# Rotary embedding on one core: a first store that begins with 1 KB of each partition

## The chip, the cores and the metric

The kernel runs on one core of one Trainium2 chip. The metric is the device time of one execution in microseconds (us); the median of several runs is compared.

## The reference

A rotary position embedding. `x` has 16 batches of 512 positions of 16 heads of 64 numbers, all float32 (33.5 MB); `cos` and `sin` have 512 x 32 numbers (64 KB each).

```python
x = x.reshape(batch, seq, num_heads, head_dim)
x1, x2 = x[..., :half_dim], x[..., half_dim:]
cos = cos[None, :, None, :]
sin = sin[None, :, None, :]
rotated = np.concatenate([x1 * cos - x2 * sin,
                          x1 * sin + x2 * cos], axis=-1)
```

So 33.5 MB are read, 33.5 MB are written, and each number takes part in two products and one sum.

## The kernel before

The 16 batches are worked on as 8 slabs of two batches' size. A slab is 128 partitions by 8192 float32, 4 MB. Two neighbouring slabs (0-1, 2-3, 4-5, 6-7) make a pair: a partition holds 64 KB of the pair, which lie next to each other in the input and in the output, and partition p's row lies 64 KB behind that of partition p-1. There are three places on the chip for a pair (`places`, the tile named `pair` in the profile), so pair 6-7 goes into the place of pair 0-1 once that is stored.

`load(s, n, parts)` brings n slabs from slab s on into their place, `store` writes them to the output; both are issued by SyncE (line 66 in the profile, where `issue` records every DMA) in the order of the program. That order is: load 0 (4 MB), cos, sin, loads 1, 2 and 3 (4 MB each), load 4-5 (8 MB); then store 0-1 in two halves, the even partitions and the odd ones, and load 6-7 in the same two halves; then stores 2-3, 4-5 and 6-7, 8 MB each. Half of load 6-7 can start when the half of store 0-1 that reads the same partitions has landed. SyncE takes its instructions one after the other: one that waits holds all behind it.

Ahead of all that ScalarE issues two DMAs of 512 bytes (line 85): from the tile `blank`, which holds zeros, to the start of the output, which store 0-1 overwrites later, and from the start of `cos` into another part of `blank`.

The tables for cos and sin are loaded into every fourth partition, spread over all partitions by eight small matmuls and kept in bfloat16 (`tabs`). A slab is then worked on in place: ScalarE casts it to bfloat16 into the lower half of its own bytes (line 154), VectorE multiplies it by the two tables (line 170, two instructions) and adds the products crosswise (line 173), and ScalarE casts the sum back to float32 (line 154). The cast of slab s+1 comes ahead of the products of slab s. Slab 0 is done in two passes and slab 7 in three, so that the first can begin and the last end early; the others are done in one. After the last cast of an odd slab, its pair is stored.

Of the kernel before, what the change touches and what calls it, by code (L numbers as in the profile page):

```python
# [2 lines left out]

# [4 lines left out]


@with_exitstack  # L10
def kernel(
    ctx: ExitStack,
    tc: tile.TileContext,
    x: bass.AP,
    cos: bass.AP,
    sin: bass.AP,
    num_heads: int,
    out: bass.AP,
):
    nc = tc.nc  # L20
    P = nc.NUM_PARTITIONS

    batch, seq, dim = x.shape
    nh = num_heads
    hd = dim // nh
    half = hd // 2
    bf16 = mybir.dt.bfloat16
    f32 = mybir.dt.float32

    nb = 2  # L30
    nslabs = batch // nb
    rpp = nb * seq // P
    W = rpp * dim
    TP = seq // (2 * rpp)
    TS = P // TP
    TW = 2 * rpp * half

    out_flat = out.rearrange("b s h d -> b s (h d)")

    singles = ctx.enter_context(tc.tile_pool(name="singles", bufs=1))  # L40
    pairs = ctx.enter_context(tc.tile_pool(name="pairs", bufs=3))
    psum = ctx.enter_context(tc.tile_pool(
        name="psum", bufs=1, space=bass.MemoryType.PSUM))


    def view(t, offset, *dims):
        return dataclasses.replace(t, offset=t.offset + offset,
                                   ap=[t.ap[0], *[list(d) for d in dims]])

    places = [pairs.tile([P, 2 * W], f32, tag="pair", name="pair") for _ in range(3)]


    def here(s, n=1):
        return view(places[s // 2 % 3], s % 2 * W, (1, n * W))


    def there(t, s, n=1):  # L60
        return bass.AP(tensor=t.tensor, offset=t.offset + s // 2 * 2 * P * W + s % 2 * W,
                       ap=[[2 * W, P], [1, n * W]])


    def issue(out, in_):
        tc.keep_in_program_order(nc.sync.dma_start(out=out, in_=in_))  # L66


    def load(s, n=1, parts=slice(None)):
        issue(here(s, n)[parts], there(x, s, n)[parts])  # L70


    def store(s, n=1, parts=slice(None)):
        issue(there(out_flat, s, n)[parts], here(s, n)[parts])


    EVEN, ODD = slice(0, P, 2), slice(1, P, 2)


    blank = singles.tile([1, 2 * P], f32, tag="blank")  # L80
    nc.vector.memset(view(blank, 0, (1, P)), 0.0)  # L81
    for i, t in enumerate((out_flat, cos)):
        far = bass.AP(tensor=t.tensor, offset=t.offset, ap=[[P, 1], [1, P]])
        near = view(blank, i * P, (1, P))
        tc.keep_in_program_order(nc.scalar.dma_start(
            out=near if i else far, in_=far if i else near))

    load(0)


    cos_sb = singles.tile([P, TW], f32, tag="cos_sb")
    sin_sb = singles.tile([P, TW], f32, tag="sin_sb")
    for t, src in ((cos_sb, cos), (sin_sb, sin)):
        nc.vector.memset(t, 0.0)  # L94
        issue(t[::TS], bass.AP(
            tensor=src.tensor, offset=src.offset, ap=[[TW, TP], [1, TW]]))

    load(1)
    load(2)
    load(3)  # L100
    load(4, 2)


    pick = singles.tile([P, 2 * P], bf16, tag="pick")
    nc.gpsimd.memset(pick, 0.0)  # L105
    for g in range(2):
        part = view(pick, g * P, (TP, P // TP), (1, TP))
        nc.gpsimd.affine_select(  # L108
            out=part, in_=part, compare_op=mybir.AluOpType.not_equal,
            fill=1.0 - 2.0 * g, base=0, pattern=[[0, P // TP], [-TS, TP]],  # L110
            channel_multiplier=1)

    tab1 = singles.tile([P, 2 * TW], bf16, tag="tab1")
    for i, t in enumerate((cos_sb, sin_sb)):
        nc.vector.tensor_copy(out=view(tab1, i * TW, (1, TW)), in_=t)  # L115

    accs, tabs = [], []
    for h in range(2):
        acc = psum.tile([P, 2 * rpp * hd], f32, tag=f"acc{h}", name="acc")
        for i in range(2):  # L120
            for f in range(2):
                nc.tensor.matmul(  # L122
                    view(acc, i * rpp * hd + f * half, (hd, rpp), (1, half)),
                    view(pick, i * f * P, (1, P)),
                    view(tab1, i * TW + h * rpp * half, (half, rpp), (1, half)),
                    start=True, stop=True)
        accs.append(acc)
        tabs.append(singles.tile([P, 2 * rpp * hd], bf16, tag=f"tab{h}", name="tab"))
    nc.vector.tensor_copy(out=tabs[0], in_=accs[0])  # L129

    passes = []
    for s in range(nslabs):
        r = 0
        for n in {0: (4, 4), nslabs - 1: (4, 2, 2)}.get(s, (rpp,)):
            passes.append((s, r, n))
            r += n


    def halves(u):
        s, r, n = u
        t = here(s).bitcast(bf16)
        return [view(t, (2 * r + i * n) * dim, (1, n * dim)) for i in range(2)]


    def cast(u):
        s, r, n = u
        copy(halves(u)[0], view(here(s), r * dim, (1, n * dim)))  # L150


    def copy(out, in_):
        tc.keep_in_program_order(nc.scalar.copy(out=out, in_=in_))  # L154


    for i, u in enumerate(passes):
        s, r, n = u
        if i == 0:
            cast(u)  # L160
            cast(passes[1])
            copy(tabs[1], accs[1])
            cast(passes[2])
        elif s > 0:
            for v in passes:
                if v[0] == s + 1:
                    cast(v)
        lo, up = halves(u)
        for t, a in ((up, 0), (lo, rpp * hd)):
            nc.vector.tensor_mul(  # L170
                out=t, in0=lo,
                in1=view(tabs[s % 2], a + r * hd, (hd, n), (0, nh), (1, hd)))
        nc.vector.tensor_add(  # L173
            out=up, in0=up, in1=view(lo, half, (hd, n * nh), (-half, 2), (1, half)))

        copy(view(here(s), r * dim, (1, n * dim)), up)
        if s == 1:
            for act in (store, load):
                for parts in (EVEN, ODD):
                    act(0 if act is store else 6, 2, parts)  # L180
        elif s % 2 and r + n == rpp:
            store(s - 1, 2)


# [1 line left out]
_INS = ['x', 'cos', 'sin', 'num_heads']  # L186
_OUTS = [((16, 512, 16, 64), 'float32')]

_NUMBERS = {'num_heads': 16}


# [26 lines left out]
```

## Time and profile before

| | |
|---|---|
| median of 3 runs | 162.09 us (161.96 to 162.14) |
| the profiled execution | 162.06 us, its span 160.3 us |
| ScalarE busy | 113.9 us (71%) |
| VectorE busy | 109.8 us (68%) |
| TensorE busy | 1.9 us (1%) |
| moved by DMA | 67.24 MB in 1572 packets, 420 GB/s over the span |

The span runs from the first to the last instruction of the program; the time of the execution also holds what lies around it. The profile calls the queue of SyncE's DMAs q1 and that of ScalarE's q10. SPq, ACTq and PEq are the instruction queues of SyncE, ScalarE and TensorE. A DMA is cut into packets, one for each partition's row here, which the 16 DMA engines move; a window's "DMA share" is the mean busy share of these engines, with each packet put where it begins, so that short windows show some unevenness (shares over 1). A packet of 4 bytes at the end of a DMA on each engine reports its completion. "Landing" is the time when all 16 reports of a DMA are in.

### The profile page before, as it was taken

Reading aid. Unit: us, or ns where it says so; the run is one execution under the profiler, and the core shown is the slowest. Engines: PE = TensorE matmul, PEld = TensorE weight load, DVE = VectorE, ACT = ScalarE, POOL = GpSimd, SP = SyncE. Lnnn points to the kernel's source line nnn. Section 1 sums busy time; section 2 is a strip of 40 time slices with the busy share of each in tenths; the row PEclk is TensorE's granted clock in tenths of the full one; section 3 lists DMA queues with packets and bytes.
Section 4 is the critical chain, followed back from the end, with each engine's and each line's share of the span. In section 5 each row is a group of like instructions: output and inputs, shape, how many; then the busy total and the mean of one; then the engine's idle time right before and its main releaser. Section 6 shows DMA issues by size and latency. Waiting matters only on the chain.

```text
span 160.3 us, 176 instructions
## 1 busy us (share of the span) xinstructions
PE 1.9 (1%) x8; PEld 1.1 (1%) x8; DVE 109.8 (68%) x39; ACT 113.9 (71%) x24; POOL 1.1 (1%) x7
## 2 busy tenths in 40 slices
PE   0004000000000000000000000000000000000000
PEld 0002000000000000000000000000000000000000
DVE  2004899999899989989998996008999998000000
ACT  3008959999999999999999900699999969400000
POOL 2000000000000000000000000000000000000000
DMA  7999999999989996996996997997997998998983
GB/s 262 393 393 450 499 393 393 499 417 393 540 376 523 393 393 262 523 507 278 523 507 278 523 474 311 523 474 311 523 458 327 523 425 360 523 409 376 523 376 147
DMA packets 1572, 67.24 MB, mean 420 GB/s; under 512 B 226, under 2 KB 228, under 8 KB 292
## 3 DMA queue, kind: packets, MB, share of 16 engines
q1 hardware_dynamic: 1568, 67.24, 98.0%
q10 hardware_dynamic: 4, 0.00, 0.0%
HBM read 33.69 MB, written 33.55 MB: 420 GB/s over the span
## 4 chain that ended last, share of the span: by engine, by line
DMA 44%; ACT 18%; DVE 15%; issue 7%; ACTq 2%; SPq 1%
DMA pair<-in_x_dram 24%; DMA out_dram<-pair 19%; ACT pair L154 18%; DVE pair L170 10%; DVE pair L173 4%; ACTq L213 1%; SPq L66 1%; DVE sin_sb L94 0%; DVE cos_sb L94 0%; DVE blank L81 0%; ACTq L154 0%
## 5 line engine op out<-in xcount | busy, mean ns | idle before, releaser
L154 ACT CAST pair<-pair 128x8192 bf16<-128x8192 f32 (+5 forms) x22 | 111.7, 5153 | 22.5 <-DMA pair<-in_x_dram 21.1
L170 DVE TENSOR_TENSOR pair<-pair,tab 128x8192 bf16<-128x8192 bf16 (+2 forms) x22 | 71.4, 3259 | 12.7 <-ACT pair L154 12.4
L173 DVE TENSOR_TENSOR pair<-pair 128x8192 bf16<-128x8192 bf16 (+2 forms) x11 | 35.8, 3259 | 0.3
L115 DVE CAST tab<-cos_sb 128x512 bf16<-128x512 f32 x1 | 0.4, 428 | 11.0 <-DMA cos_sb<-in_cos_dram 11.0
L154 ACT ACT_TABLE_LOAD x1 | 1.3, 1283 | 1.8 <-DVE cos_sb L94 1.8
L122 PE MATMUL acc<-tab,pick 128*128 128x256 bf16 x8 | 1.9, 411 | 13.6 <-DVE tab L115 13.6
L129 DVE CAST tab<-acc 128x1024 bf16<-128x1024 f32 x1 | 1.2, 1225 | 1.0 <-PE acc L122 1.0
L122 PEld LDWEIGHTS <-pick 128*128 128x128 bf16 x8 | 1.1, 136 | 13.9 <-issue 12.0
L154 ACT CAST tab<-acc 128x1024 bf16<-128x1024 f32 x1 | 1.0, 1004 | 0.0
L81 DVE MEMSET blank<- 1x128 f32 x1 | 0.2, 165 | 0.8 <-PEq L199 0.8
L108 POOL TENSOR_SCALAR_AFFINE_SELECT pick<-pick 128x128 bf16<-128x128 bf16 x2 | 0.6, 308 | 0.1
L94 DVE MEMSET sin_sb<- 128x512 f32 x1 | 0.5, 485 | 0.1
L94 DVE MEMSET cos_sb<- 128x512 f32 x1 | 0.5, 485 | 0.1
L115 DVE CAST tab<-sin_sb 128x512 bf16<-128x512 f32 x1 | 0.4, 420 | 0.0
L105 POOL MEMSET pick<- 128x256 bf16 x1 | 0.3, 311 | 0.3 <-POOLq L199 0.3
L199 POOL MEMSET const-bfloat16-1.0<- 128x1 bf16 x1 | 0.1, 101 | 0.0
L199 POOL MEMSET const-uint8-127<- 128x1 uint8 x1 | 0.1, 101 | 0.0
L199 POOL MEMSET const-float32-0.0<- 128x1 f32 x1 | 0.1, 98 | 0.2 <-issue 0.2
L199 POOL MEMSET const-float32-1.0<- 128x1 f32 x1 | 0.1, 98 | 0.0
## 6 DMA issues: line engine op xcount, KB each, us to landing
pair<-in_x_dram SPq DMA_DIRECT2D x4, 4096.0 KB, 24.6
out_dram<-pair SPq DMA_DIRECT2D x5, 24.6
cos_sb<-in_cos_dram SPq DMA_DIRECT2D x1, 64.0 KB, 11.4
sin_sb<-in_sin_dram SPq DMA_DIRECT2D x1, 64.0 KB, 11.0
pair<-in_x_dram SPq DMA_DIRECT2D x3, 19.3
out_dram<-blank ACTq DMA_DIRECT2D x1, 0.5 KB
blank<-in_cos_dram ACTq DMA_DIRECT2D x1, 0.5 KB
```

What stands on the lines that cost most here:

```text
L66: tc.keep_in_program_order(nc.sync.dma_start(out=out, in_=in_))
L94: nc.vector.memset(t, 0.0)
L105: nc.gpsimd.memset(pick, 0.0)
L108: nc.gpsimd.affine_select(out=part, in_=part, compare_op=mybir.AluOpType.not_equal, fill=1.0 - 2.0 * g, base=0, pattern=[[0, P // TP], [-T ...
L115: nc.vector.tensor_copy(out=view(tab1, i * TW, (1, TW)), in_=t)
L122: nc.tensor.matmul(view(acc, i * rpp * hd + f * half, (hd, rpp), (1, half)), view(pick, i * f * P, (1, P)), view(tab1, i * TW + h * rpp * ...
L129: nc.vector.tensor_copy(out=tabs[0], in_=accs[0])
L154: tc.keep_in_program_order(nc.scalar.copy(out=out, in_=in_))
L170: nc.vector.tensor_mul(out=t, in0=lo, in1=view(tabs[s % 2], a + r * hd, (hd, n), (0, nh), (1, hd)))
L173: nc.vector.tensor_add(out=up, in0=up, in1=view(lo, half, (hd, n * nh), (-half, 2), (1, half)))
L199: nc = _bacc.Bacc("TRN2", target_bir_lowering=False, num_devices=1)
L213: with _tile.TileContext(nc) as tc:
```

## The change

Store 0-1 becomes three DMAs in place of two: first the first 256 numbers (1 KB) of the 64 KB of each of the 128 partitions, then the remaining 63 KB of the even partitions, then those of the odd ones. Load 6-7 stays in two halves; each writes whole rows, so the even half now needs the 1 KB store and the even store to have landed, and the odd half the 1 KB store and the odd store. To this end `here`, `there`, `load` and `store` take a range `a` to `b` within the row. The 512 byte read of `cos` on ScalarE's queue is left out; the 512 byte write to the output stays.

```diff
-    def here(s, n=1):
-        return view(places[s // 2 % 3], s % 2 * W, (1, n * W))
+    def here(s, n=1, a=0, b=None):
+        b = n * W if b is None else b
+        return view(places[s // 2 % 3], s % 2 * W + a, (1, b - a))
...
-    def store(s, n=1, parts=slice(None)):
-        issue(there(out_flat, s, n)[parts], here(s, n)[parts])
+    def store(s, n=1, parts=slice(None), a=0, b=None):
+        issue(there(out_flat, s, n, a, b)[parts], here(s, n, a, b)[parts])
...
-    blank = singles.tile([1, 2 * P], f32, tag="blank")
-    nc.vector.memset(view(blank, 0, (1, P)), 0.0)
-    for i, t in enumerate((out_flat, cos)):
-        far = bass.AP(tensor=t.tensor, offset=t.offset, ap=[[P, 1], [1, P]])
-        near = view(blank, i * P, (1, P))
-        tc.keep_in_program_order(nc.scalar.dma_start(
-            out=near if i else far, in_=far if i else near))
+    SHORT = 256
+    blank = singles.tile([1, P], f32, tag="blank")
+    nc.vector.memset(blank, 0.0)
+    tc.keep_in_program_order(nc.scalar.dma_start(out=bass.AP(
+        tensor=out_flat.tensor, offset=out_flat.offset, ap=[[P, 1], [1, P]]), in_=blank))
...
         if s == 1:
-            for act in (store, load):
-                for parts in (EVEN, ODD):
-                    act(0 if act is store else 6, 2, parts)
+            store(0, 2, b=SHORT)
+            for parts in (EVEN, ODD):
+                store(0, 2, parts, a=SHORT)
+            for parts in (EVEN, ODD):
+                load(6, 2, parts)
```

## The prediction

> **What bounds the kernel now.** I read the page first, then SyncE's waits, then the time by windows, then the packet records of the trace.
>
> ```profile
> span 160.3 us, 176 instructions
> ...
> PE 1.9 (1%) x8; PEld 1.1 (1%) x8; DVE 109.8 (68%) x39; ACT 113.9 (71%) x24; POOL 1.1 (1%) x7
> ...
> q1 hardware_dynamic: 1568, 67.24, 98.0%
> q10 hardware_dynamic: 4, 0.00, 0.0%
> HBM read 33.69 MB, written 33.55 MB: 420 GB/s over the span
> ```
>
> No compute engine is above 71%, but queue q1 (all DMAs that SyncE issues) keeps the 16 DMA engines busy for 98.0% of the span. The packet records say the same from inside. Each engine starts at 1.8 to 2.4 us, then runs packet after packet with no gap until 158.4 to 159.1 us; a 64 KB packet takes 2.418 us, a 32 KB packet 1.213 us. The sum for one engine: 32 x 1.213 + 48 x 2.418 = 154.9, cos and sin with the completion packets 0.5, and 1.7 of excess that I come to, together 157.1 us, which is 98.0% of 160.3. So this is one stream of transfers, and the time changes only by what lengthens, shortens or starves that stream. 1.8 us lie around the span (162.06 for the profiled execution; the median of the three runs is 162.09, so the two agree).
>
> Does anything starve it? SyncE's waits:
>
> ```profile
> SPq L66 <- ACT pair L154: 91.4, 3, 37.5
> SPq L66 <- DMA out_dram<-pair: 29.9, 2, 20.6
> ...
> SPq L66 <- DMA pair<-in_x_dram: 8.5, 1, 8.5
> ```
>
> and its issues in the timeline:
>
> ```profile
> 50.71 1.16 SPq L66 DMA_DIRECT2D out_dram<-pair  x2
> ...
> 72.53 10.48 SPq L66 DMA_DIRECT2D pair<-in_x_dram  x2
> ...
> 83.11 55.39 SPq L66 DMA_DIRECT2D out_dram<-pair  x3
> ```
>
> The two halves of store 0-1 are issued at 50.71 and 51.3, but the stream is busy with load 4-5 and begins them at 62. The even half has landed at 72.5; load 6-7 even is issued then, 9 us before the stream has finished the odd half. Load 6-7 odd follows at 82.50, 9 us ahead as well, then store 2-3 at 83.11, 18 us ahead. These waits are long but covered.
>
> What is left to win is the excess. The windows (length, busy times, clock, DMA share, GB/s):
>
> ```profile
> 41.60:51.30 9.70, 0.00 (x0) 0.00 (x0) 9.10 (x3) 9.70 (x3) 0.00 (x0) 1.00 1.01 439
> ...
> 58.50:62.10 3.60, 0.00 (x0) 0.00 (x0) 3.57 (x2) 3.60 (x1) 0.00 (x0) 1.00 0.82 291
> 62.10:64.50 2.40, 0.00 (x0) 0.00 (x0) 2.40 (x1) 2.40 (x2) 0.00 (x0) 1.00 1.01 437
> ...
> 100.80:103.20 2.40, 0.00 (x0) 0.00 (x0) 0.00 (x0) 1.62 (x1) 0.00 (x0) 1.00 1.01 437
> ```
>
> From 58.5 to 62.1 the stream carries 291 GB/s where its neighbours carry 437. In the packet records these are the last packets of load 4-5, one on each of the 16 engines: 3.16 to 4.03 us, mean 3.59, in place of 2.42. All engines lose about 1.17 us, right ahead of the first packet of the first large store. The next turn from load to store, at 101, shows nothing (437). The other excess is at the start: the first 32 KB packet of each engine takes 1.72 in place of 1.21.
>
> **The change, part by part.**
>
> *Short store, as bytes.* Store 0-1 moves the same 8 MB. What is new is 128 packets of 1 KB, 8 for each engine. From the records, a 512 B packet took 27 ns and a 2 KB packet 84, so 0.0371 ns a byte and 8 ns fixed; 1 KB makes 46 ns. Eight are 0.37 us, plus a completion packet of 9 ns; the 8 KB that they take out of the large packets save 8 x 2.418/64 = 0.30. Net +0.08 us. A second row supports it: the loads of cos and sin, 128 KB in 2 KB packets, took 4 x 84 + 2 x 9 = 0.35 us on an engine against 0.30 at full rate. The same bytes in more packets cannot take less, so the low end is the 0.05 of the row above (a gain by the slow packet is counted below); the high end is that pieces of 1 KB written to rows 64 KB apart go badly, for which the nearest row is the slow packet, +1.2. I take 0.08, since the 512 B packet that fits the line was itself a write to the output.
>
> [...]
>
> *Short store, as an issue.* One more DMA on SyncE, some 0.5 us (two took 1.16 us), at 50.7. The even and odd halves go out at 51.2 and 51.8; the stream reaches them at 62, so 10 us hide it. Without that cover it costs 0.5.
>
> *Short store, as a wait.* Load 6-7 even must now wait for the short store and for the even half. The short one ends first, and the even half some 0.23 us later than now (0.38 of short packets less 0.15 by its four shorter rows). Behind the waiting instruction stand load 6-7 odd and store 2-3, both with 9 us or more. Cost 0.
>
> *The slow packet.* This is the part that can move the time. If the 1.17 us come from the size of the first store packet that the engines take up while the last load packet still runs, a 1 KB packet cuts them: down to -1.2. If they are a fixed cost of the first large write, they stay, and a second small-to-large step could bring a second one: +1.2. For a fixed cost: all 16 engines end the slow packet within 0.7 us (61.8 to 62.5) whenever they began it, and the turn at 101 with the same packet sizes shows nothing, so it is not size alone. I take 0.
>
> *No short read of cos.* Two packets of 27 and 9 ns on one engine, 0.04 us, and one issue of 0.23 us on ScalarE's queue at 1.54, ahead of an activation table load that ends 9.7 us before ScalarE's first data. Gain 0 to 0.04. The unknown is whether the small read at 6 us makes the real cos load at 12.0 us go smoothly: its packets show no excess. Bounds for a cold first read: nothing, up to 0.5 (start of x) or 1.2 (first store). The read went through one engine only, and sin, which nobody reads ahead, shows no excess either. I take 0.
>
> *A side effect.* Load 4-5 is the ninth DMA issued now, and SyncE waits 8.5 us for load 0 before it, although its place is empty: the DMAs seem to share eight completion semaphores in turn. With the read gone it is the eighth, and goes out near 4.7 us rather than 12.8. The stream has loads until 42 us; cost 0.
>
> *The end.* Store 6-7 is issued at 138.17 and the stream finishes store 4-5 at 139.8. The chain of waits behind that issue begins with the landing of load 6-7 odd at 101.5, which is in the same stream just ahead of stores 2-3 and 4-5, so both shift together and the 1.6 us stay.
>
> Sum: 162.06 + 0.08 - 0.00 = 162.14, call it 162.2. That is within 0.2% (0.3 us), about what a measurement of this kernel can tell from no change.
>
> **The rivals.**
>
> B, faster: the slow packet shrinks. For: it stands exactly ahead of the first large store, where the change puts small packets, and the first packets of 32 KB lost 0.5 us where the 64 KB ones lost 1.2. Against: the clustered ends and the clean turn at 101. Time 162.06 + 0.08 - 0.4 to 1.2 = 160.9 to 161.7.
>
> C, slower: the first read of cos becomes cold. The place is 12 us, between load 0 and load 1; the price 0.5 to 1.2 us on every engine, as at the start of x and of the first store; it decides as soon as load 0's last packet takes over 1.5 us. For: the clean 2 KB packets now follow a small read of the same tensor by 6 us. Against: the small write to the output at 3.6 us did not keep the first store clean, and sin is clean without help. Time 162.6 to 163.3.
>
> D, slower: the stall stays and the 1 KB writes, or the step from them to 63 KB packets, cost up to as much again: 162.5 to 163.3. Against: the 27 ns write.
>
> E, slower: load 6-7 even is held until the odd half has landed too, because the short store touches all partitions. Then the stream runs dry: 0.36 from last packet to landing, 1.02 from issue to first packet (0.73 to 1.75 at the start), 0.5 for the slow first packet, 1.9 together: 164.0. Against: the even half does not wait for the odd one today.
>
> F, slower: the short store pays its own start and landing in the stream, 1.02 + 0.36 = 1.4: 163.5. Against: cos and sin follow each other with no gap.
>
> **How the numbers follow.** A (nothing moves, 162.0 to 162.4) 0.32; B 0.30; C 0.20; D 0.10; E 0.05; F 0.03. Faster is B, 0.30; same is A, 0.32; slower is C to F, 0.38. The time is A's. The range of 8 in 10 takes in B, A, C and D, 160.9 to 163.4, and leaves out E, F and the ends of the others; A's own range is 162.0 to 162.4.
>
> **What would show it.** Right: the window ahead of the first store still near 291 GB/s; queue q1 with 1712 packets (1568 + 128 + 16), q10 with 2; load 4-5 issued near 4.7 us; load 6-7 even near 72.7; every window after 62 at 437; span near 160.4. B shows as that window at 400 or more and all later issues of SyncE about 1 us earlier. C shows as a dip at 11 to 13 us with load 0 landing late; D as a dip after 62; E as load 6-7 even issued near 82.6. Far outside would be 63 KB rows cut into many pieces: q1 with thousands of packets.

## The result and the profile after

The changed kernel takes 162.44 us (median of 9 runs, 162.32 to 162.62), the kernel before 162.03 (161.90 to 162.33) beside it: a ratio of 1.0025, 95% interval 1.0016 to 1.0033. It is slower by 0.4 us. The profiled execution took 162.39 us with a span of 160.2.

The page of the changed kernel:

```profile
span 160.2 us, 178 instructions
...
PE 1.9 (1%) x8; PEld 1.1 (1%) x8; DVE 109.7 (69%) x39; ACT 113.9 (71%) x24; POOL 1.1 (1%) x7
...
q1 hardware_dynamic: 1712, 67.24, 98.0%
q10 hardware_dynamic: 2, 0.00, 0.0%
```

The span is no longer than before: 160.2 against 160.3. The counts of packets are the forecast ones. What is longer is the time outside the span: 162.39 - 160.21 = 2.18 us here, 162.06 - 160.27 = 1.79 before.

SyncE's waits and its issues in the timeline:

```profile
SPq L68 <- DMA out_dram<-pair: 29.6, 2, 20.5
...
SPq L68 <- DMA pair<-in_x_dram: 8.1, 1, 8.1
```

```profile
2.75 2.09 SPq L68 DMA_DIRECT2D pair<-in_x_dram  x4
...
33.49 18.50 SPq L68 DMA_DIRECT2D out_dram<-pair  x3
...
72.55 10.20 SPq L68 DMA_DIRECT2D pair<-in_x_dram  x2
...
82.83 55.62 SPq L68 DMA_DIRECT2D out_dram<-pair  x3
```

Load 4-5 now goes out with loads 1 to 3 (four issues from 2.75 on, the last at 4.4). The short store goes out at 33.49, which I had put at 50.7: its 256 numbers lie in the first pass of slab 0, whose cast back ends then. The wait of 8.1 us for load 0 is now ahead of it. The early issue gains nothing, since the stream reaches the store at 62 either way. The two halves follow at 50.84 and 51.4; load 6-7 even is issued at 72.55, as before at 72.53.

The windows (length, busy times, clock, DMA share, GB/s), with the first one over the last packets of load 4-5:

```profile
58.30:61.75 3.45, 0.00 (x0) 0.00 (x0) 3.45 (x1) 3.45 (x1) 0.00 (x0) 1.00 0.98 304
62.05:64.45 2.40, 0.00 (x0) 0.00 (x0) 2.37 (x2) 2.40 (x1) 0.00 (x0) 1.00 1.08 459
...
100.80:103.20 2.40, 0.00 (x0) 0.00 (x0) 0.00 (x0) 1.67 (x1) 0.00 (x0) 1.00 1.01 437
```

The first window in the trace of before:

```profile
58.30:61.75 3.45, 0.00 (x0) 0.00 (x0) 3.45 (x1) 3.45 (x1) 0.00 (x0) 1.00 1.04 304
```

The slow packet is still there, but windows this short don't show it safely: a packet counts where it begins, and the prediction's own window, 58.5 to 62.1, gives 185 GB/s here. So the reading rests on the packet records. In them it takes 3.38 us on the mean of the 16 engines (3.60 before). The 1 KB packets take 46 ns each and the 63 KB ones 2.380 us, with no gap between them. So the stream is what the sum made of it, and the 0.4 us are not in it.

### The profile page after: what moved, and what is told of

It is laid out like the page before. It is cut to its first block, busy times and chain, and to the rows that moved or that the text cites. A ratio compares the mean times of both kernels' runs of the same rounds, so it can differ in the third digit from the quotient of the medians.

```text
span 160.2 us, 178 instructions
## 1 busy us (share of the span) xinstructions
PE 1.9 (1%) x8; PEld 1.1 (1%) x8; DVE 109.7 (69%) x39; ACT 113.9 (71%) x24; POOL 1.1 (1%) x7
## 4 chain that ended last, share of the span: by engine, by line
DMA 44%; ACT 18%; DVE 15%; issue 7%; ACTq 2%; SPq 1%
DMA pair<-in_x_dram 25%; DMA out_dram<-pair 19%; ACT pair L154 18%; DVE pair L170 10%; DVE pair L173 4%; ACTq L215 1%; SPq L68 1%; DVE sin_sb L94 0%; DVE cos_sb L94 0%; DVE blank L84 0%; ACTq L154 0%
```

## The experiments

In what follows "outside" is the time of a run less its span, as a mean over the 11 or 12 runs of each kernel; the kernel before has 1.79 in each of the four comparisons (15 to 35 runs each, single runs 1.74 to 1.84; the spans of single runs are on record to 0.1 us, which alone makes such a spread). A trace also holds instructions that only wait for semaphores (EVENT_SEMAPHORE), which the page does not count, and on VectorE three named DRAIN; with them VectorE has 53 in the kernel before and 55 in the changed one, and no other engine has a different number (SyncE 33, ScalarE 45, GpSimd 23).

**The two parts of the change, one by one.** *e1_no_read* is the kernel before without the read of cos:

```diff
-    for i, t in enumerate((out_flat, cos)):
...
-        tc.keep_in_program_order(nc.scalar.dma_start(
-            out=near if i else far, in_=far if i else near))
+    tc.keep_in_program_order(nc.scalar.dma_start(out=bass.AP(
+        tensor=out_flat.tensor, offset=out_flat.offset, ap=[[P, 1], [1, P]]), in_=blank))
```

> The kernel before without the short read of cos; store 0-1 stays in two halves of 64 KB rows. If the change's 0.4 us come with the dropped read (theory R), this run is near 162.4 with a span near 160.2, the difference lying outside the span. If they come with the short store (theory S), it is at 162.0 with 160.3. If only the number of instructions or DMAs matters (theory N), it is at or under 162.0.

Measured: ratio 1.0007 (0.9997 to 1.0016), outside 1.78, span 160.49 where before had 160.44.

*e2_short_and_read* is the changed kernel with that read kept:

```diff
-    tc.keep_in_program_order(nc.scalar.dma_start(out=bass.AP(
-        tensor=out_flat.tensor, offset=out_flat.offset, ap=[[P, 1], [1, P]]), in_=blank))
+    for i, t in enumerate((out_flat, cos)):
...
+        tc.keep_in_program_order(nc.scalar.dma_start(
+            out=near if i else far, in_=far if i else near))
```

> The kernel before with the short store of 1 KB of each partition and its two 63 KB halves, the short read of cos kept. Theory R: 162.0 to 162.1 (span 160.2 to 160.4, about 1.8 outside). Theory S: near 162.4. Theory N: at or over 162.4, with one DMA more than either kernel.

Measured: ratio 1.0025 (1.0015 to 1.0034), outside 2.19, span 160.45 where before had 160.44.

*e3_change_again* is the changed kernel, unedited.

> The changed kernel itself, unedited, beside the others on the same chip: 162.4 by every theory, span 160.2 to 160.3, about 2.15 outside the span. If it is at 162.0 here, the difference belongs to the chip and not to the program.

Measured: ratio 1.0023 (1.0014 to 1.0031), outside 2.20, span 160.38.

So the difference comes with the short store and lies outside the span; the dropped read costs nothing that these runs can tell. Theory R (the dropped read) falls. Against the kernel before, e2_short_and_read has one more instruction on SyncE (the DMA), one on ScalarE (a wait) and two on VectorE; in the changed kernel, which lacks the read, SyncE and ScalarE stand at the numbers of before. So what both slower kernels have more is one DMA with its packets, and two VectorE instructions.

**Which of these it is.** VectorE's line 170, before and after:

```profile
L170 DVEq EVENT_SEMAPHORE  x6: 21/21/1256, 14.8 to 101.5; - x6
```

```profile
L170 DVEq EVENT_SEMAPHORE  x8: 21/21/1256, 14.9 to 108.6; - x8
```

The products on slab 6 wait for DMAs that used its place. By the semaphores that the trace records there, these are the two halves of load 6-7 in the kernel before, in one waiting instruction; with the short store they are these two and all three DMAs of store 0-1, in three instructions. The two more take 21 and 50 ns, inside the span, and are hidden: VectorE waits there for ScalarE's cast in either kernel. Three kernels change the number of instructions without the short store, or the other way about.

*e4_two_on_vector*:

```diff
     nc.vector.tensor_copy(out=tabs[0], in_=accs[0])
+    spare = singles.tile([1, P], f32, tag="spare")
+    for _ in range(2):
+        nc.vector.memset(spare, 0.0)
```

> The kernel before with two more tiny VectorE instructions (writes of zeros to an unused tile, 0.17 us each, behind the tables), no short store. In the first runs the time outside the span was 1.79 us in the kernel before and without the read (53 VectorE instructions in the trace) and 2.19 with the short store (55), the spans alike. Theory V (VectorE's number of instructions adds the 0.4): 2.19 outside, 162.5 to 162.6 on this chip, ratio 1.0025. Theory D (the short DMA itself adds it): 1.79 outside, 162.2. Theory T (the number of all instructions, 178 here): 2.19.

Measured: ratio 1.0001 (0.9992 to 1.0010), outside 1.79. It decides nothing: the two instructions ran from 2.0 us on, ahead of the casts of cos and sin, the two waiting instructions in front of these casts fell away, and the trace has 53 on VectorE again.

*e5_two_on_gpsimd* is the same edit with `nc.gpsimd.memset`.

> The kernel before with the same two tiny instructions on GpSimd instead, 178 instructions in all and 53 on VectorE. Theory V: 1.79 outside the span, 162.2. Theory D: 1.79, 162.2. Theory T: 2.19, 162.6.

Measured: ratio 0.9998 (0.9989 to 1.0007), outside 1.79, 178 instructions in all. The number of all instructions (theory T) is not it.

*e6_change_two_fewer* is the changed kernel with

```diff
-    nc.vector.memset(blank, 0.0)
+    nc.gpsimd.memset(blank, 0.0)
...
-        nc.vector.memset(t, 0.0)
+        (nc.vector if t is cos_sb else nc.gpsimd).memset(t, 0.0)
```

> The changed kernel with two fewer VectorE instructions: the zeroing of blank and of sin_sb is done by GpSimd. Theory V: 1.79 outside the span, and as the span is that of the changed kernel (160.2 to 160.4), 162.1 to 162.2, level with the kernel before or 0.05 us under it. Theory D and theory T: 2.19 outside, 162.6, ratio 1.0025.

Measured: ratio 0.9997 (0.9988 to 1.0007), outside 1.79, span 160.48 where before had 160.44. Its line 170 still has the eight waits:

```profile
L170 DVEq EVENT_SEMAPHORE  x8: 21/21/1256, 14.9 to 108.9; - x8
```

The short store and its waits are all there, VectorE has 53 instructions, and the 0.4 us are gone. That takes out the DMA itself (theory D) and leaves VectorE's number of instructions.

**The number alone.** Copies of one number per partition, placed behind the tables in a fixed order so that they take over no wait (n = 2, 1 and 8):

```diff
+    spare = singles.tile([P, n], f32, tag="spare")
+    for k in range(n):
+        tc.keep_in_program_order(nc.vector.tensor_copy(
+            out=view(spare, k, (1, 1)), in_=view(tabs[0], k, (1, 1))))
```

> The kernel before with two more VectorE instructions (copies of one number per partition to an unused tile) placed so that they take over no wait: 55 in the trace, as in the changed kernel; two halves of store 0-1, no short store. Theory V (the number of VectorE instructions): 2.19 us outside the span, 162.6 on a chip where before is 162.2, ratio 1.0025. Theory W (it is not the number, but the waits on the short store's completion): 1.79 outside, 162.2.

Measured (*e8_vector_55*): ratio 1.0022 (1.0014 to 1.0030), outside 2.21, span 160.28 where before had 160.34. Its line for the products, which is line 174 there:

```profile
L174 DVEq EVENT_SEMAPHORE  x6: 21/21/50, 16.2 to 101.7; - x6
```

Theory V is shown: without any short store, with the six waits of before on its products, two more VectorE instructions cost the whole 0.4 us.

> The same with one more VectorE instruction, 54. If the 0.4 us come as a step between 53 and 55, it is 1.79 or 2.19 outside; if by 0.2 for each instruction, 1.99. Theory W: 1.79.

Measured (*e9_vector_54*): ratio 1.0013 (1.0005 to 1.0022), outside 2.05, single runs 1.98 to 2.13.

> The same with eight more VectorE instructions, 61. As a step: 2.19 outside, 162.6. By 0.2 for each: 3.4 outside, 163.8. Steps of a few instructions: 2.6 to 3.0. Theory W: 1.79.

Measured (*e10_vector_61*): ratio 1.0019 (1.0011 to 1.0027), outside 2.21, span 160.25. So the time rises from 53 to 55 and no further up to 61. With 54 it stands between: over the 1.99 of an even rise and under the full step, and no run shows why.

*e11_lean* goes the other way: the zeros are written by GpSimd, and cos and sin lie in one tile with one cast.

```diff
-    for t, src in ((cos_sb, cos), (sin_sb, sin)):
-        nc.vector.memset(t, 0.0)
+    nc.gpsimd.memset(both, 0.0)
...
-        nc.vector.tensor_copy(out=view(tab1, i * TW, (1, TW)), in_=t)
+    nc.vector.tensor_copy(out=tab1, in_=both)
```

> The kernel before with five fewer VectorE instructions, 48: GpSimd does all zeroing, cos and sin share one tile and one cast. If the step between 53 and 55 is the only one near, 1.79 outside and 162.2; if there is one for each few instructions, 1.2 to 1.6 outside and 161.6 to 162.0, under both kernels. The span should be that of before, 160.4.

Measured: ratio 0.9997 (0.9988 to 1.0005), outside 1.81, 48 on VectorE. There is no second step down to 48, and no version here beats the kernel before.

What the step is made of shows in one trace only. The DMA view of e10_vector_61 from 150 us on, beyond its span's end at 160.0, has a queue that the same view of the kernel before does not have:

```profile
q1 hardware_dynamic: 64, 3.15, 36.3%
q14 instruction: 1, 0.01, 0.1%
```

That is one fetch of instructions, 8 KB at 161.75 us in the records, and the end barrier's last semaphore events come 2.34 us after the span instead of 1.90. The Trainium skill, "Runtime: NRT & Kernel Launch", section "Instruction fetch mechanics", says that an engine's instruction memory is refilled block by block through a DMA queue of its own and that the cost of crossing into a block is mostly hidden; the fetch, on a queue of its own, agrees with the first; the 0.42 us at the end of this kernel do not look hidden. Which engine the fetch is for, the record does not tell. In the traces with 54 and 55 instructions no such fetch is recorded at the end and the last recorded events stand where they stood before, so that their 0.26 and 0.42 us are the same fetch, a little later, is argued and not shown. Packets of this kind may lack a record: ahead of the span there are 4 of 8 KB in e8_vector_55, 6 in the kernel before and 7 in e11_lean.

**The slow packet.** It was the part of the prediction that could have moved the time most. Two kernels ask what it is; in both, zeros go to places of the output that store 0-1 overwrites later. *e7_blank_all* has the early write made for all rows:

```diff
-    blank = singles.tile([1, 2 * P], f32, tag="blank")
+    blank = singles.tile([P, 2 * P], f32, tag="blank")
...
+                      ap=[[P, 1] if i else [2 * W, P], [1, P]])
+        near = view(blank, i * P, (1, P))[:1 if i else P]
```

> The kernel before with the early write of zeros to the output made by all 16 DMA engines: 512 bytes of each of 128 partitions to the start of each 64 KB row, instead of 512 bytes by one engine. If the slow packet ahead of the first large store (3.60 us in place of 2.42 on all engines) is each engine's first write to the output, it falls to 2.4 to 2.6 and the span to about 159.3, the time to 161.1. If it belongs to the first large store as such (its size, or the turn from loads to stores), it stays at 3.3 to 3.6 and the time is 162.1 to 162.4, with 0.1 for the added packets.

Measured: ratio 1.0015 (1.0006 to 1.0024), span 160.62 where before had 160.44; the last packets of load 4-5 take 3.41 us. An early write by every engine does not spare it.

*e12_store_at_42* puts such a write into the stream:

```diff
...
     load(3)
+    issue(bass.AP(tensor=out_flat.tensor, offset=out_flat.offset,
+                  ap=[[2 * W, P], [1, P]]), view(blank, 0, (1, P)))
     load(4, 2)
```

> The kernel before with one more small store in the stream, of zeros, 512 bytes of each of 128 partitions to the start of its row of the output, issued by SyncE between load 3 and load 4-5 (VectorE stays at 53 instructions, so 1.79 us outside the span). It asks what the slow packet ahead of the first store is. If it belongs to the first store of the stream on each engine, it moves to the end of load 3 at 42 us (last packets near 1.8 to 2.4 in place of 1.21 us) and the last packets of load 4-5 fall to 2.42: time 162.1 to 162.4. If each turn from loads to stores ahead of which no store has run for long costs it, both places show it: 163.2 to 163.5. If only a large store brings it, the place at 42 is clean and the one at 62 stays at 3.3 to 3.6: 162.2 to 162.4.

Measured: ratio 1.0022 (1.0011 to 1.0032), span 160.85 where before had 160.53, outside 1.78 (the added packets alone are 8 x 27 + 9 ns = 0.23 us). Two of its windows:

```profile
40.40:43.40 3.00, 0.00 (x0) 0.00 (x0) 2.87 (x1) 3.00 (x1) 0.00 (x0) 1.00 1.11 470
...
58.30:61.75 3.45, 0.00 (x0) 0.00 (x0) 3.45 (x1) 3.45 (x1) 0.00 (x0) 1.00 0.97 304
```

The turn to a store at 42 is clean (the last packets of load 3 take 1.213 us each) and the place at 58 is as slow as ever, 3.35 us in the packet records. So it is neither the first write nor the first turn from loads to a store, if a small one counts. In the fourteen traces the slow packet lies between 3.29 and 3.60 us, with the short store (3.29 to 3.44) and without (3.30 to 3.60) nearly alike. What it is stays open: the first large store, or something at that time. The second turn to a large store, at 98 to 101, is not always clean either: in nine of the fourteen traces some of the last packets of load 6-7 take 2.6 to 3.04 us in place of 2.418. Those over 2.5 us together cost an engine 0.17 to 0.23 us on the mean in e4, e6 and e7, and 0.01 in the kernel before.

## Why the prediction was right or wrong

The time lies in the range, at 0.24 us above the 162.2 and just above A's own 162.0 to 162.4. The forecast was 0.14 more than the kernel before; measured are 0.41, and the interval of 0.09% to each side tells that from no change, which the prediction did not expect of a measurement. The likeliest case was no change within 0.2%; measured is a little over that, slower, to which the cases C to F had given 0.38. None of C to F happened: what made it slower is not in the prediction, and that the time still lies in a range of 2.5 us is luck as far as these 0.4 us go.

- *Short store, as bytes* (+0.08): held. The packets took the 46 ns and 2.380 us that the sum used. The mean span with the short store is 0.01 us over that of before (e2) or 0.06 under it (e3), in e6 0.05 over, so 0.08 is not refuted and not resolved.
- *Short store, as an issue*: no cost, as said, but at 33.49 and not 50.7; I took the short store to need slab 1.
- *Short store, as a wait* (cost 0): this is the step that failed. It follows SyncE's new wait, and names who stands behind it on SyncE; there the cost is 0, with load 6-7 even at 72.55. But the pair's next users, VectorE and ScalarE, wait for the stores' completions too. VectorE's list of waits for slab 6 grew by two instructions, and these lengthen the time outside the span by 0.40 us, a term that the sum lacks. The prediction took the 1.8 us around the span as a constant; e8_vector_55 shows that it is not.
- *The slow packet* (0, bounds -1.2 to +1.2): it stayed, as taken, and B with 0.30 was not met. The reason given for it, a fixed cost of the first large write, is only half borne out: e7 and e12 exclude a first write and a first turn to a small store, and leave the large store or the time. One argument for it doesn't hold: the 16 packets do end within 0.7 us, but they also began within 0.4, so their ends don't gather at one time. The other, the clean turn at 101, holds for the trace of before, not for all. And the sign for B, its window at 400 or more, could mislead: e12_store_at_42 gives 455 there with the slow packet in place.
- *No short read of cos* (0): held. e1_no_read shows neither a cold read (C) nor a gain. The trace has the same 84 ns packets.
- *A side effect*: load 4-5 went out at 4.4 us (4.7 was said), at no cost.
- *E and F*: the even half of load 6-7 does not wait for the odd store, and the short store pays no start of its own in the stream.

## What to carry to other kernels

Set the span beside the time of the same run, for several runs, before looking into the trace: here the difference of 0.4 us was outside in every run and no view of the span could have shown it. An edit to one queue can add waiting instructions on the engines that use the same buffer later (here two on VectorE and one on ScalarE), and these count as instructions even where their waits are hidden. Where a kernel stands just below such a step, moving two instructions to another engine (e6_change_two_fewer) is worth as much as the edit cost.

## What was not expected of the hardware

The time outside the span depends on how many instructions VectorE has, waits counted: 1.78 to 1.81 us with 48 and 53 of them, 2.05 with 54, 2.19 to 2.21 with 55 and 61, while two more on GpSimd (23 to 25) left it at 1.79. Where such steps lie for other engines or larger programs was not tried.
